# Low parts of the mixing weights on GpSimd, more row buffers and longer pauses in the scan: a two-layer hybrid decoder on one core

## The chip, the cores and the metric

The kernel runs on one core of one Trainium2 chip. The metric is the device time of one execution in microseconds (us). Times shown are the median of three runs, and one further execution was taken with the hardware profiler. The engines are PE (TensorE, matrix multiply), DVE (VectorE), ACT (ScalarE), POOL (GpSimd) and SP (SyncE, which issues most transfers). Each engine has its own queue and serves it in order.

## The reference, cut to what matters

Two layers of a decoder with four token mixers are applied to 512 prompt tokens and 8 x 4 sample tokens together (544 columns). Per layer:

```
h  = rmsnorm(x) * (1 + scale1) + shift1          # scale, shift, gate from silu(c) @ w_ada + b_ada
z  = h @ w_in                                     # 1024 -> columns of four mixers and of the gates
yA = windowed means of z, per-group linear        # pooling branch
yB = retention(rotary(q), rotary(k), v)           # group norm, swish gate
yC = B * conv3(C * h_c)                           # short convolution
yD = rwkv7(z)                                     # a recurrence over tokens, see below
mixed = sum_n sigmoid(gate_n) * (y_n @ w_br[n]) @ w_out
x  = x + gate1 * mixed
h2 = rmsnorm(x) * (1 + scale2) + shift2
up = causal_dwconv3(h2 @ w_up);  x = x + gate2 * ((silu(a) * b) @ w_down)     # [a|b] = up
```

The recurrence of the rwkv branch, for every head:

```
S = S * w_t + (S a_t) b_t^T + v_t k_t^T ;   y_t = S r_t
```

It ends with a final norm. All inputs and outputs are float32; the states of every mixer are outputs too.

## The kernel before, in words

**Weights.** All weight matrices of a layer are cut into 138 units of 128 x 1024 floats, one after the other in the order of use: units 0 to 7 feed the rwkv branch, 8 to 13 the short convolution, 14 to 23 the gates and the projection of yC, 24 and 25 the pooling branch, 26 to 35 its gates, 36 to 43 retention (queries, keys, values, gate, first for the heads 0 and 1, then for 2 and 3), 44 to 53 the gates of yD, 54 to 63 those of yB, 64 to 71 w_out, 72 to 137 the feed-forward part. `load_unit` (L101) brings one in: SP issues the transfer into `raw` (3 buffers, L103), ACT rounds it to the high part `whi` (L110), and the low part `wlo = raw - whi` follows (L111). `whi` and `wlo` have 4 buffers each, so a unit can be prepared when the fourth one before it is no longer read. `getw` prepares up to 3 units ahead (2 in the gates).

**Matmuls.** `mm3` (L126) makes one product of a 128 x 128 tile with 272 columns out of three matmuls: high x high (L130), high x low (L131), low x high (L132). A unit is 8 tiles x 2 halves of the columns x 3 = 48 such wide matmuls. `split_hilo` (L372) makes the high and low parts of an operand (ACT L373, DVE L374).

**Order of work.** PE's order is that of the program text. The branches with long chains of small steps (rwkv, retention, the modulation sections `ada`) are generators that run between the wide matmuls: `mm3` counts its matmuls in `nmm` and after each three asks `slot` (L153) which generators are due. A generator yields the number of wide matmuls to let pass until its next step; since the question comes after every third, a pause is rounded up to a multiple of three. For the other engines a planner sets the order, from the dependencies and its own costs.

**The rwkv branch** (L376) is spawned when units 0 to 7 are done. Its steps: low-rank maps and norms (L392 to L422), five product steps (L428 `products`, matmuls L437, L477, L484, with pauses of 48 and 44), the solution of a triangular system by substitution on DVE (L562), and the scan: 16 chunks of 32 tokens (L628), each with three stages on PE:

- L636, copied by ACT (L639) to `gs`; pause D_G;
- L605 (`sa_of`), copied by DVE and ACT (L610, L611) into `z`; pause D_S. In every second chunk `newZ` prepares the next `z` (POOL L583 and L584, PE L593, ACT L597);
- L654 and L658, then DVE L666 adds the carried state, two L672 multiply it by the decay into the `z` of the next chunk, and POOL L673 does the same for the carry; pause D_P.

After the scan come the sample tokens, the statistics (L741, L742, L743), `ln_bones` (L362, ACT L367), the exponential (L370) and the final products (L753 to L758), which give `yD`. `finish(rw)` (L1201) would run all remaining steps at once when the second gate unit of yD has been multiplied, and the first projection reads `yD` right after it.

**Retention** (`retentions`, L860) starts when its units 36 to 39 are done and the scan is done. Each of its two passes has four steps: L773 and L780; L792 to L801; L821 to L841; L362. Its queries and keys are rotated as rows (L1181 to L1198): POOL loads two tables (L1181), ACT issues four transfers that swap the halves of the rows (L1195), DVE and POOL multiply (L1196, L1197), DVE adds (L1198).

**Buffers.** `ZR` tiles (128 x 562) are the row buffers of all branches and stages, 10 of them, also used for small tiles of 32 or 128 columns. `T4` tiles hold four rows each, 13 of them. The residual (L338) multiplies the sample part by its gate into a `ZR(32)` (L346) before it is added (L348).

Of the kernel before, what the change touches and what calls it, by code (L numbers as in the profile page):

```python
# [22 lines left out]
PAST_LEN = 4096  # L23
D_FF = 2816
NU = 138
D_G, D_S, D_P = 12, 12, 18
KAPPA = -math.exp(-0.5)

RW_UNITS = [22, 23, 18, 19, 16, 17, 20, 21]
# [14 lines left out]
def tile_hybrid_step(ctx: ExitStack, tc: tile.TileContext, io: dict):  # L44
    nc = tc.nc
# [8 lines left out]
    base = ctx.enter_context(tc.tile_pool(name="base", bufs=1))  # L54
    parp = ctx.enter_context(tc.tile_pool(name="parp", bufs=2))
    t4p = ctx.enter_context(tc.tile_pool(name="t4p", bufs=13))
    zrp = ctx.enter_context(tc.tile_pool(name="zrp", bufs=10))
    wp = ctx.enter_context(tc.tile_pool(name="wp", bufs=4))
    drp = ctx.enter_context(tc.tile_pool(name="drp", bufs=2, space=bass.MemoryType.DRAM))
    psd = ctx.enter_context(tc.tile_pool(name="psd", bufs=3, space=bass.MemoryType.PSUM))  # L60
# [4 lines left out]

    def ZR(n=562, dt=F32):
        return zrp.tile([128, n], dt, tag="zr", name=nm("zr"))

    def PM():
        return psm.tile([128, 512], F32, tag="m", name=nm("pm"))  # L70
# [30 lines left out]
    def load_unit(l, u):  # L101
        raw = wp.tile([128, 1024], F32, tag="raw", name=nm("raw"), bufs=3)
        nc.sync.dma_start(raw, io["wst"][l, u])  # L103
        dst = extra_pools.get((l, u))
        if dst is None:
            hi = wp.tile([128, 1024], F32R, tag="whi", name=nm("whi"))
            lo = wp.tile([128, 1024], F32R, tag="wlo", name=nm("wlo"))
        else:
            hi, lo = dst()
        S.copy(hi, raw)  # L110
        (G if (l, u) in ((0, 1), (0, 2)) else V).tensor_tensor(out=lo, in0=raw, in1=hi, op=SUB)  # L111
        wloaded[(l, u)] = (hi, lo)

    order = [(l, u) for l in range(L) for u in range(NU)]
# [223 lines left out]
    def residual(xt, m, ps, half, gate):  # L338
        c0, c1 = HS[half]
        npc = HALF if half == 0 else SEQ - HALF  # L340
        x = xk(xt, m)
        V.scalar_tensor_tensor(out=x[:, c0:c0 + npc], in0=ps[:, :npc], scalar=gate[:, m, 0:1], in1=x[:, c0:c0 + npc],  # L342
                               op0=MUL, op1=ADD)
        if half == 1:
            t = ZR(32)
            V.tensor_tensor(out=smp(t), in0=smp(ps[:, npc:HALF]),  # L346
                            in1=gate[:, m, 1:9].unsqueeze(2).broadcast_to([128, NB, DT]), op=MUL)
            V.tensor_tensor(out=x[:, SEQ:TOK], in0=x[:, SEQ:TOK], in1=t, op=ADD)  # L348
        return x[:, c0:c1]
# [26 lines left out]
    def rwkv(l, za, zb, M, yD):  # L376
# [83 lines left out]
            return bkv  # L460

        bkn = products(0)
        yield 48
        for T in range(5):
            n = 128 if T < 4 else 32
            nch = n // 32
            bkv = bkn
            if T < 4:
                bkn = products(T + 1)
            psA = PM()  # L470
            psB = PM()
            for c in range(nch):
                for p in range(2):
                    cc = (c * 2 + p) * 64
                    for q in range(2):
                        r = par_rows(q)
                        PE.matmul(psB[kv_rows(q), cc:cc + 64], lhsT=bkv[r, p, c].rearrange("r w t -> r (w t)"),  # L477
                                  rhs=ident[r, 64 * q:64 * q + 64], start=True, stop=True)
            for c in range(nch):
                for p in range(2):  # L480
                    cc = (c * 2 + p) * 64
                    for q in range(2):
                        r = par_rows(q)
                        PE.matmul(psA[kv_rows(q), cc:cc + 64], lhsT=bkv[r, p, c].rearrange("r w t -> r (w t)"),  # L484
                                  rhs=LG[q][r, 4 * T + c, p, :], start=True, stop=True)
            S.copy(BK[:, 4 * T:4 * T + nch, :, :].rearrange("r c p t -> r (c p t)"), psB[:, 0:nch * 128])
            mc = C_MSK if T < 4 else C_MSS
            for q in range(2):
                r = kv_rows(q)
                V.tensor_tensor(  # L490
                    out=LG[q][r, 4 * T:4 * T + nch, :, :].rearrange("r c p t -> r (c p) t"),
                    in0=psA[r, 0:nch * 128].rearrange("r (x t) -> r x t", t=64),
                    in1=cst[r, mc:mc + 64].unsqueeze(1).broadcast_to([64, 2 * nch, 64]), op=MUL)
            if T == 3:
                scr1 = drp.tile([64, 32, 32], F32, tag="scr1", name=nm("scr1"))
                for q in range(2):
                    r0 = 64 if q == 0 else 0
                    for p in range(2):
                        nc.sync.dma_start(scr1[(2 * q + p) * 16:(2 * q + p) * 16 + 16].rearrange("c s t -> s c t"),
                                          LG[q][r0:r0 + 32, 0:16, p, 0:32])  # L500
            if T < 4:
                yield 44
        rks = []
        for p in range(2):
            rk = ZR(TOK)
# [122 lines left out]
        for ch in range(16):  # L628
            T, c = ch // 4, ch % 4
            if c == 0:  # L630
                psY = PM()
                pY = psY[:, 0:256].rearrange("p (q x) -> p q x", q=2)
            psG = PM()
            for p in range(2):
                for q in range(2):
                    PE.matmul(psG[32 * q:32 * q + 32, 64 * p:64 * p + 64], lhsT=LG[q][:, ch, p, 0:32],  # L636
                              rhs=Z[q][:, c % 2, p, :], start=True, stop=True)
            gs = M["pool"].tile([64, 2, 64], F32, tag="gs", name=nm("gs"), bufs=2)
            S.copy(gs.rearrange("r p i -> r (p i)"), psG[0:64, 0:128])  # L639
            if ch == 13:  # L640
                P0 = [ZR(512) for _ in range(2)]
                for p in range(2):
                    G.dma_start(P0[p], io["s_wkv"][l, :, p])
            yield D_G
            psS = sa_of(lambda q, p: XT[32 * q:32 * q + 32, ch, p, :], gs)
            if c % 2 == 0:
                Zn = newZ(ch + 2, 2 if ch < 14 else 1)
            sa_out(psS, [Z[0][:, c % 2], Z[1][:, c % 2]])
            yield D_S
            psP = PM()  # L650
            for p in range(2):
                for q in range(2):
                    r = kv_rows(q)
                    PE.matmul(psP[par_rows(q), 64 * p:64 * p + 64], lhsT=BK[r, ch, p, :], rhs=Z[q][r, c % 2, p, :],  # L654
                              start=True, stop=True)
            for p in range(2):
                for q in range(2):
                    PE.matmul(pY[par_rows(q), p, 32 * c:32 * c + 32], lhsT=Z[q][:, c % 2, p, :], rhs=LG[q][:, ch, p, 32:64],  # L658
                              start=True, stop=True)
            pP = psP[:, 0:128].rearrange("r (p i) -> r p i", p=2)  # L660
            db = dec[:, :, ch:ch + 1].broadcast_to([128, 2, 64])
            Pt = M["pool"].tile([128, 2, 64], F32, tag="pt", name=nm("pt"), bufs=2)
            if Pn is None:
                V.tensor_copy(Pt, pP)
            else:
                V.tensor_tensor(out=Pt, in0=pP, in1=Pn, op=ADD)  # L666
            Pn = M["pool"].tile([128, 2, 64], F32, tag="pn", name=nm("pn"), bufs=2)
            if ch < 15:
                Zt, cn = (Z, 1) if c % 2 == 0 else (Zn, 0)
                for q in range(2):  # L670
                    r = par_rows(q)
                    V.tensor_tensor(out=Zt[q][r, cn], in0=Pt[r], in1=db[r], op=MUL)  # L672
            G.tensor_tensor(out=Pn, in0=Pt, in1=db, op=MUL)  # L673
            if c == 3:
                S.copy(yv[:, :, T * 128:T * 128 + 128], pY)
            if c % 2:
                Z = Zn
            if ch == 14:
                psG0 = PM()
                g0v = psG0[:, 0:128].rearrange("r (p w b t) -> r p w b t", p=2, w=2, t=DT)  # L680
                for p in range(2):
                    for b in range(NB):
                        for q in range(2):
                            r = par_rows(q)
                            PE.matmul(g0v[r, p, :, b, :], lhsT=P0[p][r, 64 * b:64 * b + 64],
                                      rhs=LG[q][r, 16, p, :].rearrange("r (w b t) -> r w b t", w=2, t=DT)[:, :, b, :],
                                      start=True, stop=True)
                g0 = ZR(128)
                S.copy(g0, psG0[:, 0:128])
                g0s = g0.rearrange("r (p w x) -> r p w x", p=2, w=2)  # L690
            yield D_P
# [70 lines left out]
    def retention(l, p, rt, M, yB):  # L762
# [36 lines left out]
        for T in range(4):  # L799
            for q in range(2):  # L800
                PE.matmul(pst[par_rows(q), 64 * T:64 * T + 64], lhsT=kt[:, T, par_rows(q)], rhs=vt[:, T, par_rows(q)],  # L801
                          start=True, stop=True)
        sms_s = ZR(32)
        V.tensor_tensor(out=sms_s[0:64], in0=ps[0:64, 0:32], in1=cst[0:64, C_RETS:C_RETS + 32], op=MUL)
        vks = ZR(128)
        S.copy(vks[0:64], pv[0:64, 0:128])
        V.tensor_copy(Sb[:, 1], pst[:, 0:64])
        for T in range(1, 4):
# [733 lines left out]
```

## Time and profile before

| | |
|---|---|
| Median of 3 runs | 1968.27 us (1968.05 to 1969.82) |
| The profiled execution | 1970.54 us, its span 1968.8 us |
| Busy: PE | 1924.9 us (98%) |
| Busy: DVE | 1046.1 us (53%) |
| Busy: ACT | 814.8 us (41%) |
| Busy: POOL | 313.3 us (16%) |
| Low parts on DVE (L111, buffers wlo) | 262 x 1239 ns |
| Low parts on POOL (L111) | 2 x 2360 ns |
| Granted TensorE clock, mean | 0.997 |

The page is of one profiled execution. In a row of the timeline stand the start and the duration in us, the engine, the line, the operation, what it writes and reads with its shape, how many were merged, and in brackets how long the engine had been idle before it and what ended that. In a row of groups stand the count, then the busy time in us and the mean in ns, then the idle time just before the group and what ended it. Matmuls are pipelined and overlap, and their ends are modelled, so the distance between two starts is the better measure of their cost. A stage in the middle of each layer, from about 200 to 345 us and from 1180 to 1316 us, has the scan between the wide matmuls.

### The profile page before, as it was taken

How to read it: one execution, taken by the hardware profiler on the slowest of the kernel's cores; microseconds unless marked ns; L12 is line 12 of the kernel's file. 1: busy time of each engine (PE TensorE's matmuls, PEld its weight loads, DVE VectorE, ACT ScalarE, POOL GpSimd, SP SyncE). 2: the span in 40 equal slices, each digit the busy share in tenths (PEclk: the TensorE clock that was granted, in tenths of full speed). 3: DMA queues.
4: the chain of work that ended last, by engine and by line, in shares of the span. 5: the costliest groups of instructions: out<-in, count | busy, mean ns of one | idle time of the engine just before them, and what ended most of it. 6: DMA issues, size and time to landing. Idle time of an engine off the chain costs nothing.

```text
span 1968.8 us, 40136 instructions
## 1 busy us (share of the span) xinstructions
PE 1924.9 (98%) x16868; PEld 1834.8 (93%) x16868; DVE 1046.1 (53%) x2017; ACT 814.8 (41%) x1531; POOL 313.3 (16%) x589
## 2 busy tenths in 40 slices
PE   5999999999999999999999999999999999999997
PEld 5989888899998889999999998889999999999997
DVE  4476443543465444555664765345335665455565
ACT  4642322452355442435445423325423555243541
POOL 1110123213000110112202101241210022011210
PEclk9999999999999999999999999999999999999999
DMA  7324333433346742222332231134224132222221
GB/s 312 98 89 130 116 111 132 161 113 96 122 147 246 305 176 87 89 93 87 119 111 87 64 110 58 63 108 122 82 78 161 52 108 86 86 87 94 89 95 47
DMA packets 75557, 227.23 MB, mean 115 GB/s; under 512 B 20208, under 2 KB 23072, under 8 KB 73584
## 3 DMA queue, kind: packets, MB, share of 16 engines
q1 hardware_dynamic: 69872, 210.43, 32.2%
q0 software_dynamic: 3536, 11.53, 1.7%
q10 hardware_dynamic: 1968, 2.69, 0.5%
q8 instruction: 133, 2.18, 0.4%
q14 instruction: 48, 0.39, 0.1%
HBM read 213.33 MB, written 9.06 MB: 113 GB/s over the span
## 4 chain that ended last, share of the span: by engine, by line
PE 91%; DVE 4%; ACT 2%; DMA 2%; issue 1%; ACTq 0%; POOL 0%; DVEq 0%; POOLq 0%
PE pd L130 28%; PE pd L132 27%; PE pd L131 26%; PE pm L220 2%; DMA raw<-in_wst 1%; ACT whi L110 1%; DVE wlo L111 1%; PE pm L654 1%; PE pm L636 1%; PE pm L605 1%; DMA zr<-zr 1%; PE pm L658 1%; PE pm L593 0%; PE pm L477 0%; PE pm L484 0%
## 5 line engine op out<-in xcount | busy, mean ns | idle before, releaser
L130 PE MATMUL pd<-t,whi 128*128 128x272 f32 x4200 | 1234.8, 294 | 3.2 <-ACT t L373 1.8
L132 PE MATMUL pd<-t,wlo 128*128 128x272 f32 x4200 | 1214.5, 289 | 0.0
L131 PE MATMUL pd<-t,whi 128*128 128x272 f32 x4200 | 1208.5, 288 | 1.0 <-DVE t L374 0.8
L130 PEld LDWEIGHTS pd<-t,whi 128*128 128x128 f32 x4200 | 790.3, 188 | 41.4 <-issue 25.7
L131 PEld LDWEIGHTS pd<-t,whi 128*128 128x128 f32 x4200 | 792.5, 189 | 2.7 <-DVE t L374 1.8
L132 PEld LDWEIGHTS pd<-t,wlo 128*128 128x128 f32 x4200 | 791.3, 188 | 0.0
L111 DVE TENSOR_TENSOR wlo<-raw,whi 128x1024 fp32r<-128x1024 f32 x262 | 324.6, 1239 | 319.6 <-ACT whi L110 319.2
L110 ACT CAST whi<-raw 128x1024 fp32r<-128x1024 f32 x264 | 276.6, 1049 | 429.9 <-PE pd L131 417.3
L1256 POOL COPY off<-zr 128x18 f32<-128x18 f32 x88 | 77.2, 878 | 556.8 <-ACT zr L1254 556.8
L342 DVE SCALAR_TENSOR_TENSOR t<-pd,mod,t 128x272 f32<-128x272 f32 (+1 forms) x160 | 77.0, 482 | 106.9 <-PE pd L132 106.8
L1093 DVE TENSOR_TENSOR zr<-pd,zr 128x272 f32<-128x272 f32 x96 | 41.2, 438 | 124.9 <-PE pd L132 124.7
L1254 ACT COPY zr<-pd 128x272 f32<-128x272 f32 (+2 forms) x264 | 72.7, 311 | 72.9 <-PE pd L132 72.9
L1108 ACT ACTIVATE zr<-pd 128x272 f32<-128x272 f32 x128 | 50.5, 394 | 105.6 <-PE pd L132 105.5
L1094 POOL TENSOR_TENSOR t<-t,zr 128x272 f32<-128x272 f32 x64 | 68.9, 1093 | 119.5 <-DVE zr L1093 119.4
L1023 DVE SCALAR_TENSOR_TENSOR zr<-zr,par,zr 128x560 f32<-128x560 f32 x92 | 73.5, 801 | 9.7 <-ACT zr L1022 9.7
L1022 ACT ACTIVATE zr<-zr,par 128x560 f32<-128x560 f32 x92 | 70.2, 765 | 17.1 <-DVE zr L1047 9.6
L1024 DVE SCALAR_TENSOR_TENSOR zr<-zr,par,zr 128x560 f32<-128x560 f32 x92 | 73.4, 801 | 2.8
L373 ACT CAST t<-zr 128x544 fp32r<-128x544 f32 (+1 forms) x96 | 49.1, 530 | 61.8 <-DVE zr L1267 61.5
L374 DVE TENSOR_TENSOR t<-zr,t 128x544 fp32r<-128x544 f32 (+1 forms) x96 | 54.1, 580 | 30.0 <-ACT t L373 29.0
L259 ACT ACTIVATE zr<-t 128x272 f32<-128x272 f32 (+1 forms) x72 | 32.0, 454 | 86.6 <-DVE t L342 55.9
L610 DVE COPY z<-pm 32x128 f32<-32x128 f32 x34 | 9.8, 289 | 69.7 <-PE pm L605 69.4
L262 DVE TENSOR_TENSOR zr<-zr,zr 128x272 f32<-128x272 f32 (+1 forms) x63 | 29.9, 475 | 20.0 <-ACT zr L259 19.3
(286 smaller groups left out, 1635.1 us busy)
## 6 DMA issues: line engine op xcount, KB each, us to landing
raw<-in_wst SPq DMA_DIRECT2D x276, 512.0 KB, 3.5
t<-in_wada SPq DMA_DIRECT2D x32, 1024.0 KB, 9.7
raw<-in_wada SPq DMA_DIRECT2D x32, 512.0 KB, 3.6
zr<-in_rope POOLq DMA_DIRECT2D x16, 272.0 KB, 3.8
t<-in_xT SPq DMA_DIRECT2D x4, 544.0 KB, 6.7
zr<-zr ACTq DMA_DIRECT2D x32, 68.0 KB, 3.2
t<-in_xT SPq DMA_DIRECT2D x2, 1088.0 KB, 6.8
xs<-t SPq DMA_DIRECT2D x2, 1088.0 KB, 4.6
```

Of the source, the lines that this page charges most:

```text
L110: S.copy(hi, raw)
L111: (G if (l, u) in ((0, 1), (0, 2)) else V).tensor_tensor(out=lo, in0=raw, in1=hi, op=SUB)
L130: PE.matmul(ps, lhsT=a, rhs=xh, start=first, stop=False)
L131: PE.matmul(ps, lhsT=a, rhs=xl, start=False, stop=False)
L132: PE.matmul(ps, lhsT=b, rhs=xh, start=False, stop=last)
L342: V.scalar_tensor_tensor(out=x[:, c0:c0 + npc], in0=ps[:, :npc], scalar=gate[:, m, 0:1], in1=x[:, c0:c0 + npc], op0=MUL, op1=ADD)
L1022: S.activation(cv, u[:, 0:560], AF.Copy, scale=wcol(0))
L1023: V.scalar_tensor_tensor(out=cv, in0=u[:, 1:561], scalar=wcol(1), in1=cv, op0=MUL, op1=ADD)
L1024: V.scalar_tensor_tensor(out=cv, in0=u[:, 2:562], scalar=wcol(2), in1=cv, op0=MUL, op1=ADD)
L1094: (V if last else G).tensor_tensor(out=a[:, c0:c1], in0=a[:, c0:c1], in1=gs, op=ADD)
L1254: pad_evac(lambda o, i, sl: S.copy(o, i), u, ps, half, 2)
L1256: G.tensor_copy(off[:, 22 * s + j], u[:, 512:562].rearrange("p (x t) -> p x t", t=2)[:, 0:25:3, :])
```

## The change

Five edits. The low part of units 0 to 63 is computed by POOL in both layers, except for units 0 and 3 of the first layer, which stay on DVE (units 1 and 2 of the first layer were on POOL already). The pauses of the scan go from 12, 12 and 18 to 16, 16 and 20, those of the product steps from 48 and 44 to 60 and 56. The row buffers go from 10 to 12. A new pool of five buffers of at most 128 columns takes the small tiles of the residual, of the scan's sample start and of retention. The descriptor scratch of software-issued transfers is set to 8192 bytes of each partition, half of the default of this compiler.

```
-D_G, D_S, D_P = 12, 12, 18
+UP0 = 64
+D_G, D_S, D_P = 16, 16, 20
...
-    zrp = ctx.enter_context(tc.tile_pool(name="zrp", bufs=10))
+    zrp = ctx.enter_context(tc.tile_pool(name="zrp", bufs=12))
+    zsp = ctx.enter_context(tc.tile_pool(name="zsp", bufs=5))
...
+    def ZS(n):
+        return zsp.tile([128, n], F32, tag="zs", name=nm("zs"))
...
         S.copy(hi, raw)
-        (G if (l, u) in ((0, 1), (0, 2)) else V).tensor_tensor(out=lo, in0=raw, in1=hi, op=SUB)
+        (G if u < UP0 and (l, u) not in ((0, 0), (0, 3)) else V).tensor_tensor(out=lo, in0=raw, in1=hi, op=SUB)
...
         if half == 1:
-            t = ZR(32)
+            t = ZS(32)
...
         bkn = products(0)
-        yield 48
+        yield 60
...
             if T < 4:
-                yield 44
+                yield 56
...
-                g0 = ZR(128)
+                g0 = ZS(128)
...
-        sms_s = ZR(32)
+        sms_s = ZS(32)
...
-        vks = ZR(128)
+        vks = ZS(128)
...
-    nc = bacc.Bacc("TRN2", target_bir_lowering=False, num_devices=1)
+    nc = bacc.Bacc("TRN2", target_bir_lowering=False, num_devices=1, dynamic_dma_scratch_size=8192)
```

## The prediction

> **What bounds the kernel now.** I read the page first (span, busy time, the chain that ended last), then the list of what PE waited for, then the timeline around each wait.
>
> ```profile
> span 1968.8 us, 40136 instructions
> PE 1924.9 (98%) x16868; PEld 1834.8 (93%) x16868; DVE 1046.1 (53%) x2017; ACT 814.8 (41%) x1531; POOL 313.3 (16%) x589
> PE 91%; DVE 4%; ACT 2%; DMA 2%; issue 1%; ACTq 0%; POOL 0%; DVEq 0%; POOLq 0%
> 800.00:850.00 50.00, 50.00 (x400) 50.00 (x400) 30.80 (x48) 23.83 (x44) 10.24 (x23) 1.00 0.30 95
> ```
>
> TensorE is the bound: 98% busy, 91% of the chain. The last row (a window in the feed-forward stage; PE first) shows the pace: 400 wide matmuls in 50 us, 0.125 us each at granted clock 1.00. The change removes no matmul, so only time in which PE stands still can be won. The waits (engine, line, what it waited for: us in total, times, longest):
>
> ```profile
> PE pm L272 <- DVE zr L262: 14.9, 2, 13.1
> ...
> PE pm L477 <- DVE zr L458: 2.8, 2, 1.4
> PE pm L636 <- DVE z L672: 1.6, 2, 0.8
> PE pd L130 <- DVE zr L346: 1.4, 1, 1.4
> PE pm L362 <- ACT zr L743: 1.2, 1, 1.2
> PE pd L131 <- DVE t L374: 0.8, 2, 0.4
> PE pm L654 <- DVE z L610: 0.6, 2, 0.3
> ```
>
> The largest, 13.1 of it in one place, is the start-up norm, which the change leaves alone. L477, L636, L346, L362 and L654, together 7.6 us, lie where it acts. They are booked too low, since the end of a matmul is modelled: distances between starts show more.
>
> ```profile
> 219.60 0.60 PE L654 MATMUL pm<-z,t 64*64 64x64 f32 x8
> ...
> 272.60 0.28 PE L132 MATMUL pd<-t,wlo 128*128 128x272 f32 x1
> 272.81 0.45 PE L654 MATMUL pm<-z,t 64*64 64x64 f32 x8
> 273.55 0.39 PE L130 MATMUL pd<-t,whi 128*128 128x272 f32 x1
> 273.70 0.60 DVE L672 TENSOR_TENSOR z<-pt,dec 64x128 f32<-64x128 f32 x2
> ...
> 233.62 1.22 DVE L111 TENSOR_TENSOR wlo<-raw,whi 128x1024 fp32r<-128x1024 f32 x1 [4.02 <-ACT whi L110]
> 234.77 0.96 DVE L1134 TENSOR_TENSOR t<-t 128x678 f32<-128x678 f32 x1
> 235.76 0.29 DVE L610 COPY z<-pm 32x128 f32<-32x128 f32 x1
> 236.10 0.73 PE L654 MATMUL pm<-z,t 64*64 64x64 f32 x8 [0.30 <-DVE z L610]
> 237.11 0.39 PE L130 MATMUL pd<-t,whi 128*128 128x272 f32 x1
> 240.44 0.65 PE L636 MATMUL pm<-z,t 128*32 128x64 f32 x7 [0.79 <-DVE z L672]
> 116.61 1.15 PE L477 MATMUL pm<-cst,zr 64*64 64x64 f32 x32 [1.39 <-DVE zr L458]
> 1277.62 0.73 PE L654 MATMUL pm<-z,t 64*64 64x64 f32 x8
> ```
>
> An undisturbed L654/L658 step costs 273.55 - 272.60 = 0.95 us between wide matmuls. At 236 it is 0.66 us more, with only 0.30 booked: DVE did a low part (L111) and L1134 before the scan's copy L610. By this distance, the scan's steps lose 6.4 us in eleven places (the first and last rows shown are two of them), the first product step 1.46 in each layer (2.9), L346 1.5, L362 1.6.
>
> **The change part by part.**
>
> ```profile
> L111 DVE TENSOR_TENSOR wlo<-raw,whi 128x1024 fp32r<-128x1024 f32 x262 | 324.6, 1239 | 319.6 <-ACT whi L110 319.2
> L111 POOL TENSOR_TENSOR wlo<-raw,whi 128x1024 fp32r<-128x1024 f32 x2 | 4.7, 2360 | 9.6 <-ACT whi L110 9.6
> 1162.83 1.22 DVE L111 TENSOR_TENSOR wlo<-raw,whi 128x1024 fp32r<-128x1024 f32 x1
> 1169.73 0.29 PE L132 MATMUL pd<-t,wlo 128*128 128x272 f32 x1
> 64.50 3.49 DVE L111 TENSOR_TENSOR wlo<-raw,whi 128x1024 fp32r<-128x1024 f32 x3
> 66.81 0.29 PE L132 MATMUL pd<-t,wlo 128*128 128x272 f32 x1
> ```
>
> *Low parts.* Of units 0 to 63 in both layers, four keep their engine, so 128 - 4 = 124 subtractions move. DVE loses 124 x 1.239 = 154 us, POOL gains 124 x 2.36 = 293 us and goes to 606, 31% of the span. Neither is the bound. What counts is whether wlo still comes before its use: the tightest unit in the steady stages (layer 1, unit 21) is done at 1164.05 and first read at 1169.73, 5.7 us later. POOL is 1.13 us slower, so 4.5 us are left: hidden, unless POOL is held longer by the work ahead of it. At the start units 4 to 6 move too: unit 4 is ready at 64.50 + 1.16, read at 66.81; POOL ends about 66.9 after its wait for DVE: +0.2 (bounds 0 and 2.4).
>
> *Contention.* Both engines slow each other:
>
> ```profile
> 405.87 1.35 POOL L1197 TENSOR_TENSOR zr<-zr,zr 128x544 f32<-128x544 f32 x1 [8.81 <-DMA zr<-zr]
> 405.94 2.36 DVE L111 TENSOR_TENSOR wlo<-raw,whi 128x1024 fp32r<-128x1024 f32 x1 [0.81 <-ACT whi L110]
> ```
>
> The DVE subtraction began 0.07 us after POOL's and took 2.36 instead of 1.24. So a moved low part can hold a DVE instruction by up to 2.36. In the scan the two L672 (both inputs in SBUF) meet it; their step has 21 x 0.125 and 0.8 for L654 and L658, 3.4 us, and the chain took 274.30 - 272.81 = 1.5, so 1.9 us are spare and only holds above that reach PE: under 0.5 us in all. The pooling branch's split L374 has nothing spare. It ends PE's wait at 265 and 1240, and a low part that starts after the cast before it ends some 0.55 later: +1.1 (0 to 4.7).
> The Trainium skill, "SBUF — State Buffer", section "Who interferes with whom", says that a DVE instruction with two SBUF inputs and a GpSimd one that reads SBUF exclude each other, and the second waits for all of the first. The 2.36 us above agree. If every moved part met it, the sum would be the 1965.8 of the third rival, against 1962.9.
>
> *Pauses.* They are counted in wide matmuls and served after every third: 12, 12, 18 become 18, 18, 21 (16 and 20 round up), 44 (45) becomes 57, 48 becomes 60. The first product step gets 12 x 0.125 = 1.5 us, what it lost: -2.9 for both layers. Scan steps get 0.75, 0.75 and 0.37 us, and most of DVE's low parts are gone from their path: I take -6.0 (bounds 0 and -6.4). The branch ends 16 x 15 + 12 + 4 x 12 + 6 = 306 matmuls, 38 us, later: at matmul 1764 after the rwkv units instead of 1458. The first use of its result is at 1728 + 96 = 1824, so no step is forced, but three things move.
>
> First, retention starts at 1734, not 1560, and gives the statistics step L362 of the scan's tail a wider gap ahead of it; the 1.6 lost at 362 goes (-1.5).
>
> ```profile
> 358.34 1.90 DVE L1196 TENSOR_TENSOR zr<-zr,zr 128x544 f32<-128x544 f32 x1 [4.32 <-DMA zr<-zr]
> 362.31 2.10 PE L362 MATMUL pm<-zr,cst 128*128 128x272 f32 x8 [1.16 <-ACT zr L743]
> DVE zr L1196 <- DMA zr<-zr: 16.1, 3, 6.8
> 371.99 1.91 POOL L1197 TENSOR_TENSOR zr<-zr,zr 128x544 f32<-128x544 f32 x1 [12.34 <-DMA zr<-zr]
> 1329.95 2.00 PE L362 MATMUL pm<-zr,cst 128*128 128x272 f32 x8
> 1346.18 1.35 DVE L374 TENSOR_TENSOR t<-t,t 128x544 fp32r<-128x544 f32 x2
> 1355.55 1.09 PE L821 MATMUL pm<-zr,t 128*64 128x128 f32 x16
> 1358.39 1.05 PE L841 MATMUL pm<-zr,zr 32*64 32x512 f32 x4
> ```
>
> Second, the scan (matmuls 747 to 1659) now lies over the rotary units, whose joins follow matmuls 1392, 1440, 1584 and 1632; before, its chunks ended at 1371. There DVE waits in order for the swapped rows (4.32, then 1.90 for L1196 beside POOL), 6.2 us with the scan's copies behind it, 4.3 more than the spare 1.9. Eight joins cost 0 to 34 us; three of the eight showed such a DVE wait, so I take 0.4 each, +3.2. The rows' swap is issued from ACT's queue, whose next scan copies wait too: inside the 1.9.
>
> Third, the tail. From L362 to the last split took 1347.53 - 1329.95 = 17.6 us with other work between. Now it has 69 x 0.125 = 8.6, plus L362 itself 1.6, plus retention's steps (L821 to the end of L841 3.9, two smaller ones by the same distance 1.8): 15.9 us. Part of that other work (two rotary joins) is gone then, so of the 1.7 missing I take 1.0 per layer, +2.0 (0 to 7).
>
> *Own small buffers and two more row buffers.* PE's one wait for L346 comes at the change of layers, where four low parts also leave DVE: -1.5 (0 to -1.5). Other row-buffer waits hold only POOL and DVE: 0. *Half the descriptor scratch:* POOL's issues take about 0.55 us and none waits visibly for space: 0 (above that, hidden until POOL is late). The modulation steps of layer 0 fire every 36 to 42 matmuls as before: 0.
>
> Sum: -(2.9 + 6.0 + 1.5 + 1.5) = -11.9; +0.2 + 1.1 + 3.2 + 2.0 = +6.5; net -5.4. The profiled execution took 1970.54 (span 1968.8), 2.27 above the median of the three runs, 1968.27; taken off the median: 1962.9.
>
> **The rivals.**
> *Rotary joins under the scan (slower).* Place and price as above; at 1.1 us a join the gain is gone, at 1.6 the kernel is slower by 0.2%. At 2.0 each: -11.9 + 3.3 + 16 = +7.4, 1975.7. For: the row at 358, where DVE's order had the join ahead of ready scan work. Against: five of eight joins show no DVE wait. 15%.
> *POOL's order holds low parts (slower).* POOL serves in order; a low part behind a wait like 12.34 is late by 12.34 - 4.5 = 7.8; two such make it 1978.5. Against: gates units come ready long before such waits would be chosen next. 8%.
> *DVE is not relieved.* If each moved part holds DVE by half its 2.36, DVE waits 124 x 1.18 = 146 of the 154 us won. Then only the pauses gain (2.9 + 3.6 + 1.5 + 1.0 = 9.0): 1968.27 - 9.0 + 6.5 = 1965.8, within 0.2%. 12%.
> *The tail is late.* Held once by 2.36 in each layer, 17.6 becomes 20.0 against 15.9: +8.2 in place of +2.0: 1969.1. 8%.
> *Nothing moves:* the waits recur elsewhere, 1968. 7%.
>
> **How the numbers follow.** My forecast has 50%, its own range 1956.4 (no cost) to 1964.3. Rivals within 0.2% (3.9 us, about what a measurement of this kernel can tell) hold 27%, slower ones 23%. The range 1955 to 1977 takes in all but the worst of the joins and of POOL's order.
>
> **What would show it.** After: L477, L346 and L362 gone from PE's waits, L636 and L654 near zero, L111 on POOL about 2.4 us each, no wlo among PE's releasers, and PE waits for L374 at the first projections of the rwkv branch below 2 us. Wrong if new PE waits name L610, L672 or L673 at the rotary units, or if L132 waits for POOL.

## The result, and the profile after

The changed kernel takes 2036.87 us (median of four runs, 2029.26 to 2040.69) against 1969.05 us for the kernel before on the same chip: ratio 1.0339, 95% interval 1.0307 to 1.037, some 68 us slower. Four more runs of it, later, gave 2032.92 and a ratio of 1.0331 (1.0313 to 1.0349). The forecast was 1962.9, faster, with a range up to 1977. It was wrong in sign. The changed kernel's lines are those of the kernel before plus 5 (L111 is L116, L130 is L135, L374 is L379, L610 is L615, L672 is L677, L1093 is L1098).

From the page of the changed kernel, the line of its engines and that of the chain:

```profile
PE 1950.4 (96%) x16868; PEld 1853.2 (91%) x16868; DVE 1007.6 (50%) x1893; ACT 817.2 (40%) x1533; POOL 574.6 (28%) x713
PE 84%; DVE 8%; ACT 3%; DMA 2%; issue 2%; POOL 1%; ACTq 0%; SPq 0%; DVEq 0%; POOLq 0%
```

The matmuls are the same, the span grew by 58.7 us, and DVE's share of the chain doubled from 4% to 8%. What PE waited for (us in total, times, longest):

```profile
PE pm L641 <- DVE z L677: 8.4, 8, 2.1
PE pd L135 <- DVE zr L1098: 8.1, 2, 4.3
PE pd L135 <- DVE t L1096: 8.0, 3, 3.3
...
PE pd L135 <- DVE zr L1052: 5.9, 2, 2.9
...
PE pm L659 <- DVE z L615: 3.9, 3, 2.7
...
PE pd L135 <- DVE zs L351: 2.4, 2, 2.2
```

Every one shown is a wait for DVE, the engine that was given less work, and the steps L641 and L659 that the longer pauses were to free are among them. (Left out are, among others, the start-up's two of 14.7 and 6.6 us, which the kernel before has in much the same size, and 3.2 us for ACT's cast L378.) The wait for wlo, at PE's weight loads, is 0.2 us in all. The groups show why: first of the changed kernel, then of the kernel before (busy us, mean ns).

```profile
L116 POOL TENSOR_TENSOR wlo<-raw,whi 128x1024 fp32r<-128x1024 f32 x126 | 305.9, 2430 | 372.6 <-ACT whi L115 368.9 <-DVE zs L351 3.5
L116 DVE TENSOR_TENSOR wlo<-raw,whi 128x1024 fp32r<-128x1024 f32 x138 | 168.9, 1224 | 204.8 <-ACT whi L115 202.6 <-DMA raw<-in_wst 1.9
L1099 DVE TENSOR_TENSOR t<-t,zr 128x272 f32<-128x272 f32 x32 | 33.3, 1045 | 0.7
L677 DVE TENSOR_TENSOR z<-pt,dec 64x128 f32<-64x128 f32 x60 | 32.8, 546 | 2.0
L426 DVE SCALAR_TENSOR_TENSOR t<-t 128x544 f32<-128x544 f32 x4 | 8.1, 2019 | 0.0
```

```profile
L672 DVE TENSOR_TENSOR z<-pt,dec 64x128 f32<-64x128 f32 x60 | 20.4, 339 | 1.8
L1094 DVE TENSOR_TENSOR t<-t,zr 128x272 f32<-128x272 f32 x32 | 13.8, 437 | 0.3
L421 DVE SCALAR_TENSOR_TENSOR t<-t 128x544 f32<-128x544 f32 x4 | 2.9, 717 | 0.0
```

The same instructions on the same shapes take up to 2.8 times as long. DVE lost 324.6 - 168.9 = 155.7 us of low parts, yet its busy time fell only from 1046.1 to 1007.6, by 38.5. So 117.2 us came back as longer instructions: I call this DVE's lengthening. One such place, in the scan of layer 0 (POOL, DVE and PE of the changed kernel):

```profile
360.46 2.84 POOL L116 TENSOR_TENSOR wlo<-raw,whi 128x1024 fp32r<-128x1024 f32 x1
361.19 2.69 DVE L1203 TENSOR_TENSOR t<-zr,zr 128x544 f32<-128x544 f32 x1
363.91 0.29 DVE L615 COPY z<-pm 32x128 f32<-32x128 f32 x1
364.26 0.78 PE L659 MATMUL pm<-z,t 64*64 64x64 f32 x8 [2.74 <-DVE z L615]
```

POOL's low part began at 360.46. DVE's L1203, 0.72 us long where nothing disturbs it, began 0.73 later, and ended when POOL had ended (363.3) and 0.6 more. Behind it in DVE's queue stood the scan's copy L615, and PE waited 2.74 us.

The second part is the clock. The mean granted clock, before and after:

```profile
core 0: 1968.8 us, clock 0.997
core 0: 2027.5 us, clock 0.986
```

Lost clock is (1 - 0.997) x 1968.8 = 5.9 us before and (1 - 0.986) x 2027.5 = 28.4 after: 22.5 of the 58.7 us. The rest, 36, is standing still and longer steps. A stall of 2.34 us that ended at 190.88, by stretches of 1 us (busy us of the engines, then the granted clock as the third number from the end):

```profile
190.00:191.00 1.00, 0.12 (x1) 0.12 (x2) 0.96 (x5) 0.00 (x0) 0.00 (x0) 1.00 0.30 119
191.00:192.00 1.00, 1.00 (x9) 1.00 (x10) 0.93 (x5) 0.00 (x0) 0.00 (x0) 1.00 0.00 0
192.00:193.00 1.00, 1.00 (x7) 1.00 (x6) 0.90 (x4) 0.00 (x0) 0.00 (x0) 0.52 0.00 0
...
195.00:196.00 1.00, 1.00 (x8) 1.00 (x7) 0.86 (x5) 0.39 (x1) 0.00 (x0) 0.78 0.00 0
```

About 1.1 us after PE had resumed, its clock was halved for 3.4 us: 1.7 us lost behind a stall of 2.3.

### The profile page after: what moved, and what is told of

Its sections match the earlier page's. It is cut to its first block, busy times and chain, and to the rows that moved or that the text cites. A ratio compares the mean times of both kernels' runs of the same rounds, so it can differ in the third digit from the quotient of the medians.

```text
span 2027.5 us, 40098 instructions
## 1 busy us (share of the span) xinstructions
PE 1950.4 (96%) x16868; PEld 1853.2 (91%) x16868; DVE 1007.6 (50%) x1893; ACT 817.2 (40%) x1533; POOL 574.6 (28%) x713
## 4 chain that ended last, share of the span: by engine, by line
PE 84%; DVE 8%; ACT 3%; DMA 2%; issue 2%; POOL 1%; ACTq 0%; SPq 0%; DVEq 0%; POOLq 0%
PE pd L135 26%; PE pd L137 25%; PE pd L136 25%; PE pm L225 2%; DMA raw<-in_wst 1%; DVE t L569 1%; DVE t L379 1%; DMA zr<-zr 1%; ACT whi L115 1%; DVE t L571 1%; PE pm L641 1%; DVE z L677 1%; PE pm L659 1%; PE pm L482 1%; PE pm L663 0%
## 5 line engine op out<-in xcount | busy, mean ns | idle before, releaser
L135 PE MATMUL pd<-t,whi 128*128 128x272 f32 x4200 | 1242.6, 296 | 27.5 <-DVE zr L1098 8.1
L135 PEld LDWEIGHTS pd<-t,whi 128*128 128x128 f32 x4200 | 797.6, 190 | 70.1 <-issue 34.1
L116 POOL TENSOR_TENSOR wlo<-raw,whi 128x1024 fp32r<-128x1024 f32 x126 | 305.9, 2430 | 372.6 <-ACT whi L115 368.9
L116 DVE TENSOR_TENSOR wlo<-raw,whi 128x1024 fp32r<-128x1024 f32 x138 | 168.9, 1224 | 204.8 <-ACT whi L115 202.6
L1098 DVE TENSOR_TENSOR zr<-pd,zr 128x272 f32<-128x272 f32 x96 | 41.9, 439 | 158.3 <-PE pd L137 157.9
L1028 DVE SCALAR_TENSOR_TENSOR zr<-zr,par,zr 128x560 f32<-128x560 f32 x92 | 78.1, 850 | 12.8 <-ACT zr L1027 12.8
L1027 ACT ACTIVATE zr<-zr,par 128x560 f32<-128x560 f32 x92 | 70.4, 766 | 22.1 <-DVE zr L1052 14.7
L379 DVE TENSOR_TENSOR t<-zr,t 128x544 fp32r<-128x544 f32 (+1 forms) x96 | 59.4, 636 | 36.8 <-ACT t L378 35.6
L1029 DVE SCALAR_TENSOR_TENSOR zr<-zr,par,zr 128x560 f32<-128x560 f32 x92 | 73.6, 801 | 3.0
L378 ACT CAST t<-zr 128x544 fp32r<-128x544 f32 (+1 forms) x96 | 49.0, 530 | 64.4 <-DVE zr L1272 64.1
L1099 POOL TENSOR_TENSOR t<-t,zr 128x272 f32<-128x272 f32 x64 | 47.8, 766 | 15.3 <-DVE zr L1098 15.1
L615 DVE COPY z<-pm 32x128 f32<-32x128 f32 x34 | 9.8, 289 | 78.4 <-PE pm L610 78.2
```

What stands on the lines that cost most here:

```text
L116: (G if u < UP0 and (l, u) not in ((0, 0), (0, 3)) else V).tensor_tensor(out=lo, in0=raw, in1=hi, op=SUB)
L135: PE.matmul(ps, lhsT=a, rhs=xh, start=first, stop=False)
L379: V.tensor_tensor(out=lo, in0=src, in1=hi, op=SUB)
L1027: S.activation(cv, u[:, 0:560], AF.Copy, scale=wcol(0))
L1028: V.scalar_tensor_tensor(out=cv, in0=u[:, 1:561], scalar=wcol(1), in1=cv, op0=MUL, op1=ADD)
L1029: V.scalar_tensor_tensor(out=cv, in0=u[:, 2:562], scalar=wcol(2), in1=cv, op0=MUL, op1=ADD)
```

## The experiments

**The runs in one table.** Lengthening is DVE's busy time over that of before, with the low parts that DVE no longer does taken off. Lost clock is (1 - granted clock) x span, less the 5.9 of before (its last digit is worth 2 us). Where no low parts moved and nothing was added on POOL, the lengthening is left empty: it is within 2 us of nothing.

| run | what it has | median, us | ratio, 95% interval | lengthening | lost clock |
|---|---|---|---|---|---|
| changed kernel | everything | 2036.87 | 1.0307 to 1.037 | 117 | 22 |
| e2 | moved low parts alone | 2017.08 | 1.023 to 1.026 | 105 | 18 |
| f1 | moved parts, buffers | 2017.27 | 1.0231 to 1.0262 | 109 | 14 |
| e1 | pauses, buffers | 1974.90 | 1.0015 to 1.0038 | | 2 |
| d1 | unneeded POOL subtraction beside all | 2052.11 | 1.0407 to 1.0436 | 159 | 29 |
| d2 | two POOL fills instead | 1969.13 | 0.9991 to 1.0009 | -1 | 0 |
| f2 | moved parts in eight pieces | 2009.83 | 1.0196 to 1.0224 | 48 | 12 |
| d1p | unneeded subtraction in eight pieces | 2049.10 | 1.0367 to 1.0418 | 67 | 29 |
| d3 | unneeded subtraction, whi only | 2017.31 | 1.023 to 1.026 | 123 | 12 |
| d3p | the same in four pieces | 1995.00 | 1.0116 to 1.0146 | 66 | 2 |
| d3c | unneeded copy of whi | 1980.11 | 1.0041 to 1.0074 | 49 | 0 |
| m1 | moved parts of units 14 to 43 | 2003.91 | 1.0152 to 1.018 | 56 | 10 |
| g44 | everything, units 44 to 63 on DVE | 2025.91 | 1.0276 to 1.031 | 83 | 18 |
| b1 | buffers alone | 1966.50 | 0.9972 to 0.9989 | | 0 |
| p1 | buffers, product pauses | 1967.18 | 0.9982 to 1.0 | | 0 |
| p3 | buffers, scan pauses | 1979.34 | 1.0029 to 1.0056 | | 0 |
| p2 | scan pauses alone | 1983.54 | 1.0058 to 1.0083 | | 4 |

Two theories stood at the start. Lock: a POOL instruction that reads SBUF holds DVE's instructions with two SBUF inputs, DVE then comes late for PE, and the clock drops after each stall. Pauses: the later scan and retention collide with rotary joins and with the gates of yD.

**Which part costs (e1, e2, f1).** e1 is the changed kernel with `UP0` taken back, f1 with the old pauses, e2 the kernel before with one line changed:

```
-        (G if (l, u) in ((0, 1), (0, 2)) else V).tensor_tensor(out=lo, ...
+        (G if u < 64 and (l, u) not in ((0, 0), (0, 3)) else V).tensor_tensor(out=lo, ...
```

> The changed kernel with its low parts back on DVE (as before: units 1 and 2 of layer 0 alone on POOL): the longer pauses, the buffers and the scratch by themselves. Lock theory (a moved low part on POOL holds DVE's instructions with two SBUF inputs, DVE then comes late for PE, and a half clock follows each stall): without the moved parts 1960 to 1966 us, none of the waits for L1098, L1096, L1052 over 2 us, at most two stretches of granted clock 0.5. Pause theory (the scan now lies over the rotary joins, and retention under the gates of yD): 1990 us or more, and the waits for L1096 and L1098 stay.

> The kernel before with only the 124 low parts moved to POOL; old pauses, old buffers. Lock theory: 40 to 65 us slower (2008 to 2034), DVE's L374 and L1093 lengthened, PE waiting for DVE at the evacuations of the gates, and ten or more stretches of granted clock 0.5. Pause theory: 1965 to 1972.

> The changed kernel with the old pauses (12, 12, 18; 48 and 44): moved low parts, buffers and scratch. The parts add up to 68 us only with some 16 to spare (moved parts alone +47, pauses and buffers alone +5). If the pauses bring moved low parts and chains together, this run is at 2010 to 2018, as the moved parts alone. If buffers or scratch make the moved parts worse (POOL starts them earlier, into more of DVE's work), 2025 or more.

The moved parts alone cost 47.3 us (2017.08 - 1969.82), within the lock theory's range and against the pause theory. f1 costs the same, so buffers and scratch do not make it worse. e1 fits neither: 5.1 us slower, where the lock theory had 4 to 10 us faster and the pause theory 20 slower. PE's waits in e2, and after them in e1:

```profile
PE pd L130 <- DVE t L1091: 7.9, 7, 2.5
PE pm L636 <- DVE z L672: 7.2, 4, 3.1
...
PE pm L477 <- DVE zr L458: 6.2, 2, 3.1
```

```profile
PE pd L135 <- DVE zr L1098: 5.5, 2, 2.8
...
PE pd L135 <- ACT t L378: 3.2, 3, 1.4
...
PE pm L641 <- DVE z L677: 0.4, 1, 0.4
PE pm L659 <- DVE z L615: 0.3, 1, 0.3
```

In e2 the old waits are longer, and L1091 at the gates is new. In e1 the waits of the first product step are gone and those of the scan all but gone, as forecast, but two waits of 2.7 and 2.8 for L1098 stand in the gates of yD.

**Is it the hold, without anything needed on POOL? (d1, d2)** Both are the kernel before, low parts on DVE, with half the descriptor scratch and with extra work on POOL whose result nobody reads (the code is shortened):

```
+  G.tensor_tensor(out=dum, in0=raw, in1=hi, op=SUB)      # d1: units 4 to 63 (0 to 63 in layer 1)
+  G.memset(raw, 0.0); G.memset(raw, 0.0)                 # d2: the same units, after lo
```

> The kernel before, its low parts on DVE, and for the same 124 units (less 0) a second subtraction raw minus whi on POOL into a tile that nobody reads (half the scratch too). It adds work that no result waits for. Lock theory: DVE is held although POOL does nothing that is needed, 30 to 70 us slower, with the moved rows of the changed kernel lengthened in the same way. A theory in which the moved low part itself is late, or in which the order of POOL's needed work matters: 0 to 10 us slower.

> The kernel before, its low parts on DVE, and for the same 124 units two fills of the raw tile with zeros on POOL after the low part has been read: POOL is busy, but it only writes SBUF. By the lock theory in the form that only a POOL instruction that reads SBUF holds DVE: within 5 us of before, DVE's rows not lengthened. If any POOL work holds DVE: 30 us or more slower. The later release of raw could cost up to 5 us.

d1 costs 82 us, d2 nothing: ratio 1.0000. POOL's added busy time is 356.7 us in d1 (670.0 - 313.3) and 223.0 in d2 (536.3 - 313.3). DVE's own low parts and the scan's L672 in d1, then in d2, with d2's fills:

```profile
L111 DVE TENSOR_TENSOR wlo<-raw,whi 128x1024 fp32r<-128x1024 f32 x262 | 411.3, 1570 | 291.9 <-ACT whi L110 283.1 <-PE pm L403 7.6 <-DMA raw<-in_wst 0.9
L672 DVE TENSOR_TENSOR z<-pt,dec 64x128 f32<-64x128 f32 x60 | 34.1, 569 | 1.8
```

```profile
L111 DVE TENSOR_TENSOR wlo<-raw,whi 128x1024 fp32r<-128x1024 f32 x262 | 324.5, 1239 | 324.3 <-ACT whi L110 324.0
L672 DVE TENSOR_TENSOR z<-pt,dec 64x128 f32<-64x128 f32 x60 | 19.9, 332 | 1.7
L112 POOL MEMSET raw<- 128x1024 f32 x248 | 235.9, 954 | 327.3 <-DVE wlo L111 300.6 <-issue 21.7 <-ACT zr L1186 0.2
```

The fills start after DVE's own low part of the same unit, so the rows of L672, which has two inputs in SBUF and which the fills do meet, weigh more: 339 ns before, 332 beside fills, 569 beside subtractions. L1093, which has one input in PSUM, keeps its mean in d1 (436 against 438 before). Nor did the planner's order change: DVE and ACT run the same instructions in the same order in d1 and d3 as before. So it isn't that POOL is busy, nor that its low part is late: POOL's reading lengthens DVE, its writing does not. The Trainium skill, "SBUF — State Buffer", section "Who interferes with whom", says just this: a DVE instruction with two SBUF inputs contends with a GpSimd one that reads SBUF and not with one that only writes. The means of both lines agree, 1570 against 1239 ns and 569 against 332.

**Length of a hold or sum of reading? (f2, d1p, then d3, d3p, d3c)** First the moved and the unneeded subtraction were cut into eight of 128 columns.

> The kernel before with the same 124 low parts on POOL, each cut into eight subtractions of 128 columns. Lock theory (one instruction holds the other engine for its whole length): a hold is at most one piece, an estimate of 0.3 to 0.4 us from 2.36 / 8 and a start, so DVE's rows L1094, L672 and L374 return to near their old means and the time is within 15 us of before. If POOL and DVE share the way to SBUF in proportion to what they read: as much slower as with whole low parts, 40 us or more.

> As the run with the unneeded second subtraction on POOL (low parts stay on DVE, +82 us), but that subtraction is cut into eight of 128 columns. Nobody waits for POOL's result, so the order of needed work on POOL can't be the cause this time. Lock theory: one hold is at most one piece, about 0.42 us (3.38 for eight in the run with pieces), so DVE's lengthening shrinks to a third or less and the time is 5 to 30 us above before. Shared-bandwidth theory (POOL's reading slows DVE in proportion): 60 us or more, since POOL reads as much as with whole ones.

Both of my times failed: 40 and 78 us slower, where the theory of shared bandwidth had put them. Yet DVE's lengthening did fall, from 105 to 48 and from 159 to 67. The reason for the rest is partly seen. Eight pieces cost POOL more (means of 0.51 and 0.63 us each against 2.45 and 3.0 for a whole one, so 4.1 and 5.0 a unit), and raw comes free later. ACT's waits for the transfer into raw, before and in d1p:

```profile
ACT whi L110 <- DMA raw<-in_wst: 7.6, 3, 3.7
```

```profile
ACT whi L110 <- DMA raw<-in_wst: 72.0, 20, 9.2
```

Behind L110 in ACT's queue stand evacuations and scan copies. In f2 that wait is 25.1, and how much of its 40 us came this way stayed open. The test was mended by reading whi alone, which POOL's delay does not keep from anyone in time (in d3 ACT's wait for raw is 8.8 us):

```
+  G.tensor_tensor(out=dum, in0=hi, in1=hi, op=SUB)       # d3;  d3p: four times 256 columns
+  G.tensor_copy(out=dum, in_=hi)                          # d3c
```

> Before, low parts on DVE, and for the same units an unneeded subtraction whi minus whi on POOL, which does not touch raw. Lock theory: POOL's reading alone costs, so most of the 82 us of the run that read raw stays: 45 to 85 us. If that run paid mainly for a late raw: under 20.

> The same subtraction of whi in four pieces of 256 columns. If the length of one hold sets the price (one piece takes an estimate of 0.6 to 0.75 us, from 2.36 / 4 and a start): DVE's lengthening a third of that with whole ones, and at most half of the time lost. If all reading counts: as much lost as with whole ones, or more.

> The unneeded work is one POOL copy of whi, so POOL reads one SBUF input, not two. If any POOL instruction that reads SBUF holds a DVE instruction with two SBUF inputs: slower in proportion to the copy's length against the subtraction's, 15 us or more. If two inputs on POOL are needed for a hold: within 5 us of before, as with the fills.

POOL's rows in d3, d3p and d3c (count, busy us, mean ns):

```profile
L112 POOL TENSOR_TENSOR dum<-whi 128x1024 f32<-128x1024 f32 x124 | 302.6, 2440 | 375.6 <-ACT whi L110 356.3 <-ACT z L611 18.4
```

```profile
L112 POOL TENSOR_TENSOR dum<-whi 128x256 f32<-128x256 f32 x496 | 437.1, 908 | 292.4 <-ACT whi L110 267.1 <-ACT z L611 24.6
```

```profile
L112 POOL COPY dum<-whi 128x1024 f32<-128x1024 f32 x124 | 201.0, 1621 | 426.9 <-ACT whi L110 426.5
```

Quarters read the same bytes, keep POOL busy 44% longer in sum (437.1 against 302.6 us) and cost half: 25.8 us against 48.1, with DVE's lengthening 66 against 123. So the length of one hold counts, not the sum. "A third" of the lengthening was too bold, and "at most half" of the time was just missed (0.54). These means contain POOL's own waits for DVE, for the hold goes both ways (where DVE's low part began first, POOL's subtraction took up to 3.0 us): the shortest took 1.88 us whole, 0.60 a quarter and 1.03 for the copy, so the estimate for a piece, 0.6 to 0.75, was right. The copy, with one input, costs 10.9 us and lengthens DVE by 49: one input is enough to hold. I had 15 or more, in proportion to length; 1.03 / 1.88 of 48.1 would be 26. The price falls faster than the length, which would fit a spare that PE's steps have, below which a hold is free; that is argued, not shown. The lost clock goes the same way, 12 us for d3 and 2 and 0 for the short ones.

**Where is it paid? (m1, g44)**

> The kernel before with the low parts of units 14 to 43 alone moved to POOL (60 of the 124): those that are prepared while product steps, scan and rotary units run. By the delay at each matmul of the run with all 124 (about 18 us from the 768th to the 1920th of layer 0, about 17 in the same stretch of layer 1, out of 45.7): if the price is paid where DVE's small steps sit on PE's path, 30 to 38 us for half of the moved parts. If each moved part costs the same wherever it is: 22 us. If it is paid at the starts of the layers and in the gates after the scan: under 15.

> The changed kernel with the low parts of units 44 to 63 back on DVE in both layers; the rest of the change as it is. If the parts meet at the gates of yD (moved part beside retention and the evacuations L1098): 5 to 16 us faster than the changed kernel, and the waits for L1098 back at 2.7 and 2.8 or below. If they meet in the scan or at the change of layers: within 3 us of the changed kernel.

> The changed kernel once more, beside the run without the late units: 2029 to 2041, as its first four runs.

m1 moves 60 of the 124 and costs 32.6 of e2's 47.3 us: paid where the small steps of the rwkv branch sit on PE's path. The start of the same wide matmul in both traces shows it place by place (us later than before; a negative number with longer pauses is mostly work put off, which comes back):

| wide matmul | before, at us | e2 | e1 | changed |
|---|---|---|---|---|
| 576th | 129.7 | +2.9 | -4.2 | -1.7 |
| 1344th | 263.0 | +14.3 | -8.7 | +3.1 |
| 1920th | 375.9 | +20.8 | -14.9 | +2.4 |
| 2304th | 444.5 | +19.4 | +4.7 | +27.9 |
| 6336th | 983.2 | +19.7 | +2.1 | +25.7 |
| 7104th | 1091.3 | +25.4 | +1.5 | +29.3 |
| 9024th | 1420.4 | +45.6 | +3.4 | +58.1 |

e2 pays in the product steps and the scan of both layers and some 6 us at the change of layers, and nothing from the 1920th matmul of a layer on. The parts sum to 47 + 5 = 52, the whole is 64 to 68. With the late units back on DVE (g44) it is 7.0 us faster than the changed kernel beside it (2032.92 - 2025.91), L1098 is back at 5.5 in total, and lost clock falls from 24.6 in that second profile to 18. So about 7 of the 12 to 16 us come from the moved parts of units 44 to 63, where they meet retention under the gates of yD; the rest stayed open.

**What the pauses cost (b1, p1, p2, p3).**

> Before with the buffers and with the longer pauses of the product steps alone (60 and 56); the scan's pauses stay 12, 12, 18, the low parts stay on DVE. By the waits removed (first product step 2.9, L346 1.5) and a branch that ends only 60 matmuls, 7.5 us, later: 1964 to 1968. If retention under the gates of yD is reached by that already: 1970 to 1975, as with all pauses.

> Before with the longer pauses of the scan alone (16, 16, 20). The scan's steps win up to 6 us; if the two waits of 2.8 us for L1098 at the gates of yD and the longer ones at the first projections of the pooling branch come from the scan's end moving 31 us, they stay and the time is 1967 to 1973; if they come from the product steps' pauses or the buffers, 1962 to 1965.

> Before with the two more row buffers, the own small buffers and half the scratch alone; old pauses, low parts on DVE. The one wait it removes is L346 (1.4 at the change of layers): 1966 to 1970, at most 0.1% faster. If the kernel with longer product pauses owes its gain to the buffers: 1964 to 1966.

> The longer pauses of the scan (16, 16, 20) with the buffers; product pauses as before. The longer scan pauses without the buffers cost 14 us, with buffers and longer product pauses together 5. If the row buffers are what the later retention lacked: 1972 to 1977. If the product pauses' later start was what helped (the scan's end falls elsewhere against the rotary joins): 1980 to 1985.

The buffers alone are 4.8 us faster by the medians (1966.50 against 1971.32, 0.1 to 0.3%): L346 is gone and the wait at the first product step fell from 2.8 to 1.1. That is the best kernel of the study. Longer product pauses on top give 1967.18: no more than the buffers alone. The scan's pauses cost 14 us alone, 8 with the buffers, 5 with buffers and product pauses. So neither account of p3 holds: its time lies between the two. The buffers take 6 off the 14, hardly more than the 4.8 that they save by themselves, so they do little against the collision as such; the product pauses take off another 3. My time for p2 (1967 to 1973) failed by over 10 us, since in e1 the savings of the buffers and product pauses had stood against the collision. What a later scan runs into, in p2 (its longest new wait, then a join) and then in e1:

```profile
PE pm L801 <- ACT t L774: 4.1, 2, 2.3
```

```profile
1355.45 1.34 POOL L1197 TENSOR_TENSOR zr<-zr,zr 128x544 f32<-128x544 f32 x1 [7.19 <-DMA zr<-zr]
1355.53 1.85 DVE L1196 TENSOR_TENSOR zr<-zr,zr 128x544 f32<-128x544 f32 x1 [3.19 <-ACT zr L1186]
1357.41 0.69 DVE L712 TENSOR_TENSOR zr<-z,cst 64x512 f32<-64x512 f32 x1
...
1358.24 0.61 PE L726 MATMUL pm<-zr,t 64*64 64x512 f32 x1 [1.17 <-DVE zr L712]
```

```profile
428.53 1.28 DVE L789 TENSOR_TENSOR zr<-pm,cst 128x512 f32<-128x512 f32 x2
429.73 0.78 DVE L1098 TENSOR_TENSOR zr<-pd,zr 128x272 f32<-128x272 f32 x2
430.21 0.39 PE L135 MATMUL pd<-t,whi 128*128 128x272 f32 x1 [2.72 <-DVE zr L1098]
```

In p2 retention's step L801 waits for ACT's copy L774; p3 has the same 4.1 us, e1 none. And a rotary join, held by POOL's half of the same join, stands ahead of the scan's tail. In e1 retention's second pass (L789) stands ahead of the evacuation that frees PE's accumulator.

## Why the prediction was wrong

*The step that failed* is the contention term: "so 1.9 us are spare and only holds above that reach PE: under 0.5 us in all". The lock was read rightly from the two rows at 405.9, and the range of one hold too. But 2.36 - 1.9 is what one hold can cost, and it was taken for all of them; the spare was taken from the scan's own chain of one step, and only its L672 were thought to be hit. A hold of 2.4 us strikes any two-input instruction ahead in DVE's queue (joins, splits, substitution, gate sums), and all share the one spare. The row at 361.19 shows it: the join was held and the scan's copy paid, in a wait that names L610 (now L615) at a rotary unit, as the prediction's own sign of being wrong has it. The sum had 0.2 + 1.1 for the moved parts and nothing for the scan; moved alone, they cost 47.3 us (e2).

*The rival "DVE is not relieved"* had the mechanism and nearly its size: 146 us of DVE time lost again, measured 117. Its error was to let it end at nothing won. DVE's mean load never bound PE; winning it gave nothing, and losing it in lumps of 2 us cost, because each lump lands on one instruction.

*The granted clock* was priced at nothing. It made 22.5 of 58.7 us.

*Right:* wlo was late once, by 0.2 us at the start, as in the sum; the split's +1.1 (L379 has 1.8 us booked in the changed kernel, L374 had 0.8); POOL's mean of 2.43 us (2.36 used); the waits L477 and L362 vanish and L636 and L654 all but vanish with longer pauses (e1), and L346 with the buffers (b1). With moved parts L351, L641 and L659 came back, since they wait for DVE.

*Mis-sized:* the tail, +2.0 in the sum. e1 shows 5.5 booked at L1098, a place the sum did not name. Another 1.4 at L378 (3.2 against 1.8 for L373 before) is not the tail's: it stands at the first projections of the pooling branch, at 256.44 and 1233.61, and p1 and p2 have it too. The joins, +3.2, cost nothing visible in e1, and appeared only in p2 and where POOL held them. The buffers gave 4.8 by themselves (b1), where the sum had 1.5. Pauses and buffers together were to give -11.9 + 5.2 = -6.7; they gave +5.1.

## What to carry to other kernels

Do not offload from DVE to GpSimd by busy shares. Where DVE has instructions with two SBUF inputs, each reading GpSimd instruction is a possible stop of up to its whole length; compare that length with the smallest spare between a DVE instruction and the matmul that waits behind it in the queue, and if the work must go there, keep pieces shorter than that spare and mind what the pieces cost GpSimd. A test costs one run: put the same reading on GpSimd as unneeded work. A pause that hides one wait moves everything behind it, so look at what stands at the place where the chain will end.

## What was not expected of the hardware

Half clock came in whole helpings: in the changed kernel thirteen stretches lost 1.7 us each, one of them twice that. Eleven came with or within 2.4 us of stalls of 1.4 to 4.3 us, but not each such stall has one: 2.37 us at 1199.98 had none, 2.34 at 190.88 had.

The traces say why. The thirteen stretches begin on one grid with steps of 3.413 us: 192.03, 256.89 and 270.54 are 19 and 4 steps apart, and all thirteen fit within 0.01 us. Of the 2.34 us, 2.26 lie within one step; a border of the grid, at 1198.97, cuts the 2.37 us into 1.36 and 1.01. Each of the 19 traces has such a grid of its own. From 41 us after the start to 14 us before the end, PE stood still for 1.9 us or more in 81 steps of them, and half clock followed in the next step 81 times; below that it went either way.

The other two of the thirteen, near 390 and 1390, follow this row in each layer, 64 matmuls of 8 columns (L690):

```profile
386.85 2.03 PE L690 MATMUL pm<-t,zr 64*64 64x8 f32 x64
```

PE shows busy there, and the clock fell all the same. The one such stretch of the kernel before, at 332, follows the same instruction (L685 there, at 329.55). In its second layer a border at 1301.77 cuts the same work, which begins at 1301.46, and no half clock follows. The Trainium skill, "TensorE: Matmul & The Clock Gate", section "Part 1: The HAM clock gate (the "warmup" mystery)", describes a free-running window of about 3.4 us and a half clock after an idle one. The length of the stretches agrees, and so does the grid; but here 1.9 us of standstill within a window were enough.

Cutting an instruction on POOL is dear: the shortest whole one of d3 took 1.88 us, and the shortest quarter in d3p 0.60, not 0.47. And the changed kernel's two profiles differ by 8.8 us of span (2027.5 and 2036.3), 2 of them lost clock. Two waits of 2.8 and 2.9 us, at 202.24 and 209.89, stand in the second alone; what they hang on stayed open.
